# A channel shuffle through PSUM: tiles of 24 KB in eight buffers instead of tiles of 32 KB in six

## The chip, the cores and the metric

The kernel runs on one core of a Trainium2 chip. The metric is the device time of one execution in microseconds (us). The profiled span of the core is about 1.8 us shorter than the device time; spans are compared with spans, and times with times.

## The reference

```python
batch, h, w, c = 16, 64, 64, 256          # groups = 8
x = x.reshape(batch, h, w, groups, c // groups)
x = x.transpose(0, 1, 2, 4, 3)            # swap group and channel-in-group
x = x.reshape(batch, h, w, c)
```

Each run of 256 floats is permuted in itself. 67.1 MB are read and 67.1 MB are written.

## The kernel before

A tile of q rows per partition is q KB a partition (one row is 256 floats, 1 KB). Each tile is loaded by a DMA that SyncE (SP) issues. It is permuted in pieces of 8 KB: VectorE copies a piece into PSUM with the permuted access pattern, ScalarE (ACT) copies it back into the same place. Then ScalarE issues the store. The store therefore stands in ScalarE's own instruction stream: while it waits to be issued, ScalarE copies nothing.

```python
_SIZES = [8] + [32] * 14 + [24, 8, 8, 8, 8]      # KB a partition
_BUFS = 6
_PIECE = 8
# ...
for q in _SIZES:
    buf = pool.tile([P, biggest * c], F32, name="buf")
    nc.sync.dma_start(out=buf[:, : q * c], in_=rows(x_flat, first, q))
    for k in range(0, q, _PIECE):
        piece = buf[:, k * c : (k + _PIECE) * c]
        bounce = psum.tile([P, _PIECE * c], F32, name="bounce")
        nc.vector.tensor_copy(
            out=bounce.rearrange("p (i j g) -> p i j g", j=CPG, g=G),
            in_=piece.rearrange("p (i g j) -> p i j g", g=G, j=CPG),
        )
        nc.scalar.copy(out=piece, in_=bounce)
    nc.scalar.dma_start(out=rows(out_flat, first, q), in_=buf[:, : q * c])
    first += P * q
# ... (launch)
```

The semaphores are not in the source: the Tile framework inserts them.

## Time and profile before

| | before |
|---|---|
| device time, median of the first 3 runs | 320.13 us (319.8 to 320.82) |
| profiled span | 317.8 us |
| VectorE busy / ScalarE busy | 72% / 38% |
| DMA engines at work (packet durations summed, over 16) | 312.4 us |

From the page of the kernel before: the 40 slices of the span (busy tenths; GB/s moved), the chain that ended last, and the two costly groups (busy us, mean ns of one, then idle us just before them and what ended it).

```profile
...
DVE  3199999893975939679395893939849497980471
...
DMA  8999999999999999999999999999999999999995
GB/s 330 406 434 413 429 429 449 408 458 417 445 429 429 445 412 458 400 462 425 433 434 425 449 408 454 429 437 429 429 446 412 442 443 438 418 417 439 413 403 215
...
DVE 59%; DMA 23%; another core or an unknown queue 15%; issue 1%; ACT 1%; SPq 0%; DVEq 0%
...
L54 DVE COPY bounce<-buf 128x2048 f32<-128x2048 f32 x64 | 228.2, 3633 | 83.0 <-DMA buf<-in_x_dram 83.0
L58 ACT COPY buf<-bounce 128x2048 f32<-128x2048 f32 x64 | 119.4, 1865 | 186.9 <-DVE bounce L54 186.9
...
```

The DMA row stays at 9 until the last slice. VectorE leads the chain, but it waits 83.0 us for loads. So the DMA engines bound the kernel, and with the same bytes to move only the two ends can be shortened.

The end of the kernel before, by stretches of time (columns: stretch in us, its length, busy us and instructions of VectorE, ScalarE and GpSimd, clock, DMA share, GB/s; a packet is counted in the stretch in which it starts, so a share can pass 1):

```profile
...
290.00:306.00 16.00, 6.85 (x2) 1.86 (x1) 0.00 (x0) 1.00 0.97 414
306.00:310.00 4.00, 2.71 (x2) 1.86 (x1) 0.00 (x0) 1.00 0.87 367
310.00:314.00 4.00, 1.26 (x1) 1.86 (x1) 0.00 (x0) 1.00 0.40 164
314.00:318.00 4.00, 0.00 (x0) 0.00 (x0) 0.00 (x0) 1.00 0.63 262
...
```

From 310 to 314 us the DMA engines are busy 40%: they wait for VectorE and ScalarE to finish the last small tile before its store can start. The packet records show no packet at all from 311.8 to 314.0 us.

### The profile page before, as it was taken

To read this page: it belongs to the slowest core of one execution; us is meant where nothing else is said; L and a number is where in the kernel's file an instruction comes from. 1 tells how busy PE (TensorE), PEld (TensorE's weight loads), DVE (VectorE), ACT (ScalarE), POOL (GpSimd) and SP (SyncE) were. 2 spreads that over 40 slices of the span, in tenths; PEclk is the share of its full clock that TensorE was granted. 3 is DMA by queue.
4 is the path that set the end of the run, shared out by engine and by line. 5 is a ranking of instruction groups with operands and counts; after the bars stand their busy time and mean duration, and the time that the engine had idled before them with its cause. 6 is when DMAs were issued, how large, how long until landed. Compare 5 with 4: busy or idle time off the path is not lost.

```text
span 317.8 us, 277 instructions
## 1 busy us (share of the span) xinstructions
DVE 228.2 (72%) x64; ACT 120.7 (38%) x65; POOL 0.2 (0%) x4
## 2 busy tenths in 40 slices
DVE  3199999893975939679395893939849497980471
ACT  1225545453351524424244252542505345242222
POOL 0000000000000000000000000000000000000000
DMA  8999999999999999999999999999999999999995
GB/s 330 406 434 413 429 429 449 408 458 417 445 429 429 445 412 458 400 462 425 433 434 425 449 408 454 429 437 429 429 446 412 442 443 438 418 417 439 413 403 215
DMA packets 5762, 134.24 MB, mean 422 GB/s; under 512 B 640, under 2 KB 640, under 8 KB 640
## 3 DMA queue, kind: packets, MB, share of 16 engines
q1 hardware_dynamic: 2880, 67.11, 49.4%
q10 hardware_dynamic: 2880, 67.11, 49.0%
q14 instruction: 2, 0.02, 0.0%
HBM read 67.11 MB, written 67.11 MB: 422 GB/s over the span
## 4 chain that ended last, share of the span: by engine, by line
DVE 59%; DMA 23%; another core or an unknown queue 15%; issue 1%; ACT 1%; SPq 0%; DVEq 0%
DVE bounce L54 59%; DMA buf<-in_x_dram 13%; DMA out_dram<-buf 9%; ACT buf L58 1%; SPq L50 0%; DVEq L54 0%
## 5 line engine op out<-in xcount | busy, mean ns | idle before, releaser
L54 DVE COPY bounce<-buf 128x2048 f32<-128x2048 f32 x64 | 228.2, 3633 | 83.0 <-DMA buf<-in_x_dram 83.0
L58 ACT COPY buf<-bounce 128x2048 f32<-128x2048 f32 x64 | 119.4, 1865 | 186.9 <-DVE bounce L54 186.9
L58 ACT ACT_TABLE_LOAD x1 | 1.3, 1283 | 5.6 <-DMA buf<-in_x_dram 5.6
L77 POOL MEMSET const-bfloat16-1.0<- 128x1 bf16 x1 | 0.1, 102 | 0.0
L77 POOL MEMSET const-uint8-127<- 128x1 uint8 x1 | 0.1, 101 | 0.0
L77 POOL MEMSET const-float32-0.0<- 128x1 f32 x1 | 0.1, 99 | 0.2 <-issue 0.2
L77 POOL MEMSET const-float32-1.0<- 128x1 f32 x1 | 0.1, 98 | 0.0
## 6 DMA issues: line engine op xcount, KB each, us to landing
buf<-in_x_dram SPq DMA_DIRECT2D x14, 4096.0 KB, 61.9
out_dram<-buf ACTq DMA_DIRECT2D x14, 4096.0 KB, 35.7
buf<-in_x_dram SPq DMA_DIRECT2D x5, 1024.0 KB, 35.2
out_dram<-buf ACTq DMA_DIRECT2D x5, 1024.0 KB, 9.9
buf<-in_x_dram SPq DMA_DIRECT2D x1, 3072.0 KB, 59.2
out_dram<-buf ACTq DMA_DIRECT2D x1, 3072.0 KB, 18.8
```

Of the source, the lines that this page charges most:

```text
L54: nc.vector.tensor_copy(out=bounce.rearrange("p (i j g) -> p i j g", j=CPG, g=G), in_=piece.rearrange("p (i g j) -> p i j g", g=G, j=CPG),)
L58: nc.scalar.copy(out=piece, in_=bounce)
L77: nc = _bacc.Bacc("TRN2", target_bir_lowering=False, num_devices=1)
```

## The change

The intent: the same 192 KB a partition, cut into more and finer buffers, and nearly all tiles of one size.

```diff
-_SIZES = [8] + [32] * 14 + [24, 8, 8, 8, 8]
-_BUFS = 6
+_SIZES = [24] * 20 + [8, 24]
+_BUFS = 8
```

## The prediction

> **What bounds the kernel now.** The DMA engines. The page shows their busy share at 9 tenths in every slice but the first and last; they move 433 to 436 GB/s from 100 to 260 us. The Trainium skill ("DMA: Bandwidth & Descriptors", "Where 436 GB/s comes from") puts the ceiling at 435 GB/s: this trace agrees. VectorE is busy 72%, ScalarE 38%. VectorE heads the chain of waits with 59%, but waits 83.0 us for loads: a 32 KB tile costs it 14.26 us, the DMA engines about 19.4 us (load and store). VectorE matters only where the DMA engines run dry.
>
> Summed over the trace's packet records and divided by 16, the DMA engines work 312.4 of the 317.8 us. They start at 1.74 us, lose some 0.5 us on slow first packets, and run dry only after the last load lands (307.6 us): 308 to 311 us partly, 312 to 314 us entirely, some 3 us together.
>
> **What the change does.** Bytes, VectorE and ScalarE work stay the same (64 pieces of 3.63 and 1.87 us). One packet is one partition row of a tile. A 32 KB packet takes 1213 ns, a 24 KB one 912, an 8 KB one 309. Per engine: before 3584x1213 + 256x912 + 1280x309 ns over 16 = 311.0 us; after 5376x912 + 256x309 over 16 = 311.4 us. So +0.4 us, all critical.
>
> Capacity in flight is the same (192 KB a partition), and each 24 KB tile costs VectorE 10.7 us against 14.6 us of DMA. So no starving in the middle. Start: the first load is 3 MB instead of 1 MB, so the first VectorE copy starts near 10 us instead of 5.5, but seven more loads keep the DMA engines busy: no effect.
>
> **The end decides.** Before, the last tile is 8 KB: from landing to store issue 5.6 us, then 1 MB of store. After, the last tile is 24 KB: three copies 10.75 us, ScalarE 1.9, issue and first packet about 1.6, together 14.3 us, then 3 MB of store alone, 7.3 us, and about 1 us to finish. The stores still queued when the last load lands cover it. The Trainium skill (same page, "Queues, rings and completion order") says that an engine round-robins between queue rows packet by packet; the trace agrees: with equal packets both queues get 216 GB/s, and from 270 to 300 us loads of 8 KB packets get about 90 against 340 for the stores of larger packets. Following packets that way with the trace's durations (estimate), one 24 KB and one 8 KB store are left when the last load lands (near 297.5 us): 9.8 us of work. So the DMA engines stand idle about 4.5 us, against 3 before: +1.6 us.
>
> **Sum.** 0.4 + 1.6 = +2.0 us: 322.1 us, range 320.6 to 323.5. Chances: faster by over 2% 0.02, within 2% 0.95, slower 0.03.
>
> **What would show it.** Load and store each near 216 GB/s from 60 to 270 us; packets of 912 ns; VectorE waiting for a load before each tile, some 4 us; the last load landing at 296 to 299 us; one DMA gap of 4 to 5 us just before the last 3 MB store; then 7.3 us of store alone.
>
> **What would make it wrong.** If the store queue held more when the last load lands, the gap closes and the time falls to 318 or less. If 24 KB rows ran at a different speed in bulk than the 256 packets of this trace, every per cent is 3 us. If the load queue empties before stores return buffers, a gap appears near 25 to 60 us.

## The result, and the profile after

| | before | after |
|---|---|---|
| device time, median of 6 runs each | 320.10 us (319.67 to 320.82) | 317.61 us (317.54 to 317.81) |
| ratio | | 0.992 (0.9907 to 0.9934) |
| profiled span | 317.8 us | 315.9 us |
| DMA engines at work | 312.4 us | 313.1 us |
| idle time of the DMA engines after 290 us | 4.0 us | 1.8 us |
| end of the last packet of the last load | 306.9 us | 285.7 us |

A ratio is the mean time of one kernel's fast runs over that of the other's of the same rounds, so it is not quite the ratio of the medians. The last three rows are summed from the trace's packet records.

The change is faster by 0.8%: inside the 2% band, as predicted, but with the opposite sign, and outside the stated range. The same parts of the page after:

```profile
...
DVE  0699999959587685957008986999970299999900
...
DMA  8999999999999999999999999999999999999997
GB/s 296 439 442 380 436 429 433 433 439 433 423 442 433 426 442 426 426 442 426 433 436 427 433 436 436 433 426 437 433 423 448 423 429 444 429 423 433 439 432 302
...
DVE 54%; another core or an unknown queue 23%; issue 8%; ACT 5%; DMA 3%; DVEq 1%; ACTq 0%
...
L54 DVE COPY bounce<-buf 128x2048 f32<-128x2048 f32 x64 | 227.9, 3636 | 72.6 <-ACT buf L58 38.8
L58 ACT COPY buf<-bounce 128x2048 f32<-128x2048 f32 x64 | 119.0, 1866 | 171.1 <-DVE bounce L54 115.3
...
```

and the same stretches at the end:

```profile
...
290.00:306.00 16.00, 10.53 (x3) 7.36 (x4) 0.00 (x0) 1.00 0.98 420
306.00:310.00 4.00, 0.00 (x0) 0.00 (x0) 0.00 (x0) 1.00 1.05 451
310.00:314.00 4.00, 0.00 (x0) 0.00 (x0) 0.00 (x0) 1.00 0.93 399
...
```

The gap before the last store is gone: after 302.5 us no engine computes, and the DMA engines only empty a queue of stores. The DVE row holds something new: two holes of "00" and "02" in mid-kernel, where VectorE stands still although the kernel is faster. The table of waits of the kernel after (engine, line, waited for: us in total, times, longest) says for what:

```profile
...
ACT buf L58 <- DVE bounce L54: 115.3, 56, 5.6
ACT buf L58 <- DMA buf<-in_x_dram: 55.7, 4, 26.0
DVE bounce L54 <- ACT buf L58: 38.8, 4, 18.8
DVE bounce L54 <- DMA buf<-in_x_dram: 33.9, 7, 11.1
...
```

Before, the second and third of these lines do not exist:

```profile
...
ACT buf L58 <- DVE bounce L54: 186.9, 64, 9.7
DVE bounce L54 <- DMA buf<-in_x_dram: 83.0, 18, 7.9
ACT L58 <- DMA buf<-in_x_dram: 5.6, 1, 5.6
...
```

ScalarE's copies read PSUM and need nothing from a later load. Yet ScalarE waits 55.7 us for loads, and VectorE, whose two PSUM buffers are then full, 38.8 us for ScalarE. The longest of these waits in the timeline of the kernel after (start, us, what; in brackets the idle time before it):

```profile
...
136.89 1.86 ACT L58 COPY buf<-bounce 128x2048 f32<-128x2048 f32 x1 [1.68 <-DVE bounce L54]
140.71 7.10 DVE L54 COPY bounce<-buf 128x2048 f32<-128x2048 f32 x2 [3.86 <-DMA buf<-in_x_dram]
164.29 0.34 ACTq L59 DMA_DIRECT2D out_dram<-buf  x1
164.72 3.63 ACT L58 COPY buf<-bounce 128x2048 f32<-128x2048 f32 x2 [25.97 <-DMA buf<-in_x_dram]
...
```

The copies of tile 9 (counted from 0) end at 138.75 us, but its store is issued only at 164.29 us. What it waits for is named in the built program, not in the source. These are lines of its instruction listing, shortened, with the semaphores that each instruction waits for (buf_171 is tile 9, buf_207 is tile 12; the wait for DMAHW2_49 stands in a small instruction just before, and both wait for its value 48, the third landing on it, after the loads of tiles 2 and 7 that of tile 12):

```
DVE  L54 TensorCopy bounce_209<-buf_207 128x2048 [waits DMAHW2_49,Activation_49]
ACT  L59 DMACopy out_0_dram<-buf_171 128x6144 [waits DMAHW2_49,Activation_49]
```

The framework deals eight completion semaphores to the program's 44 DMAs, and a DMA waits until the DMA before it on the same semaphore has landed. The Trainium skill ("DMA: Bandwidth & Descriptors", "Why a DMA increments its semaphore by 16 and not by 1") says why two DMAs in flight must not share one: the count cannot tell whose parts have arrived; "One semaphore per in-flight slot, not one per stream." No run here shows a wrong count, but the trace shows the price of the wait. The store of tile 9 shares its semaphore with the load of tile 12, whose last packet ends at 163.89 us; 0.40 us later the store is issued. The stores of tiles 10, 11 and 15 are held in the same way (by the loads of tiles 13, 14 and 18). In the kernel before, three stores (tiles 8, 9 and 15) share a semaphore with the load of the next tile, but those loads have landed in time: ScalarE waits for no load there except the first.

The theory follows, still to be tested. While stores are held, the loads have the DMA engines to themselves. Summed from packet records, from 150 to 200 us the loads move 253 GB/s and the stores 180. The engines lose nothing meanwhile: their share is 1.01 from 138 to 164 us, during the longest hold. The stores that are kept back are done at the end, where otherwise the engines would stand idle until the last tile is copied. So, by this theory, an accidental wait moved work from where it was plentiful to where it was missing.

Rivals: the queues themselves favour loads with these tile sizes; the 24 KB packets or the eight buffers bring the gain; or long stretches of loads alone, or stores alone, run faster in themselves.

### The profile page after: what moved, and what is told of

Same layout as the page of the kernel before. It is cut to its first block, busy times and chain, and to the rows that moved or that the text cites. A ratio compares the mean times of both kernels' runs of the same rounds, so it can differ in the third digit from the quotient of the medians.

```text
span 315.9 us, 289 instructions
## 1 busy us (share of the span) xinstructions
DVE 227.9 (72%) x64; ACT 120.3 (38%) x65; POOL 0.2 (0%) x4
## 4 chain that ended last, share of the span: by engine, by line
DVE 54%; another core or an unknown queue 23%; issue 8%; ACT 5%; DMA 3%; DVEq 1%; ACTq 0%
DVE bounce L54 54%; ACT buf L58 5%; DMA buf<-in_x_dram 3%; DVEq L91 1%; ACTq L59 0%; DVEq L54 0%; ACTq L58 0%
## 5 line engine op out<-in xcount | busy, mean ns | idle before, releaser
L54 DVE COPY bounce<-buf 128x2048 f32<-128x2048 f32 x64 | 227.9, 3636 | 72.6 <-ACT buf L58 38.8
```

Source lines behind the costliest of these rows:

```text
L54: nc.vector.tensor_copy(out=bounce.rearrange("p (i j g) -> p i j g", j=CPG, g=G), in_=piece.rearrange("p (i g j) -> p i j g", g=G, j=CPG),)
```

## The experiments

All twelve runs gave correct results. They ran in three batches; each batch has its own runs of the kernel before.

| run | what it is | time, us | ratio to before | end of last load, us | DMA idle after 290 us |
|---|---|---|---|---|---|
| e1 | the change, no store shares a semaphore with the load of a later tile | 320.19 | 0.9999 | 294.9 | 4.4 |
| e2 | e1 + store 9 waits for tile 12 by data | 317.78 | 0.9925 | 290.3 | 1.8 |
| e3 | e1 + store 9 waits for tile 11 by data | 320.11 | 0.9996 | 294.7 | 4.4 |
| e4 / e10 | before + store 8 waits for tile 11 by data | 317.72 / 317.80 | 0.9931 / 0.9914 | 302.8 / 301.0 | 3.2 / 1.7 |
| e11 | control of e10 without the wait | 320.00 | 0.9987 | 307.1 | 4.2 |
| e9 | the change again | 317.60 | 0.9926 | 286.1 | 2.0 |
| e5 | e1 with the 8 KB tile last | 317.61 | 0.9926 | 295.0 | 2.1 |
| e6 | the change with six buffers | 320.37 | 1.0007 | 295.0 | 4.7 |
| e8 | sixteen tiles of 32 KB | 318.19 to 320.33 (fast) | 0.9967 | 284.0 | 2.9 |
| e7 | tiles of 16 KB, twelve buffers | 321.52 | 1.0038 | 272.1 | 4.2 |
| e12 | tiles of 16 KB, eight buffers, as e1 dealt | 318.76 | 0.9948 | 296.7 | 1.6 |

About 1.1 to 1.4 us of the last column is the time from the last packet to the end of the span, which every kernel has.

### e1: the same instructions, other semaphores

```diff
-    with _tile.TileContext(nc) as tc:
+    with _tile.TileContext(nc, schedule_with_timeline_sim=True) as tc:
```

The option makes the framework order its bookkeeping by another estimate. The instructions of every engine are the same and in the same order (the two built programs were compared); only the semaphores are dealt differently, so that the store of tile 9 waits for nothing but its own copies. The expectation below says that a store never shares a semaphore with a load. The built program is not quite so: most stores share one with a load, but with that of their own or an earlier tile, which has landed, so no store waits for a load. The waits of the loads change too (in the kernel after, the loads of tiles 6 and 7 wait for those of tiles 1 and 2, 21.5 us in all; in e1 no load waits for a load), so e1 alone does not single out the held stores; e2 and e10 put a single hold back.

> The changed kernel with every instruction in the same order on every engine; only the completion semaphores are dealt out differently, so that a store never shares one with a load. Theory (some stores of the changed kernel are held back until a later load on the same semaphore has landed; that keeps stores for the end): without the holds ScalarE never waits for a load before a store, the last load's last packet ends near 297 us instead of 285.7, the DMA engines stand idle 4 to 5 us before the last 3 MB store, span 319.5 to 320.7 us, time 321.3 to 322.4 us, ratio to before about 1.005. Rival (the DMA queues themselves favour loads, or the tile size alone shifts work to the end; the semaphores do not matter): time stays 317.6 us, ratio 0.992, last load near 286 us.

Measured: 320.19 us. The gain is gone, and the rival that knows no semaphores, with its 317.6 us, falls. In the table of waits of e1, ScalarE waits for no load except the first (11.3 us); VectorE waits 78.9 us for loads again; the gap is back:

```profile
...
DVE bounce L54 <- DMA buf<-in_x_dram: 78.9, 17, 11.3
ACT buf L58 <- DMA out_dram<-buf: 13.8, 2, 6.9
ACT L58 <- DMA buf<-in_x_dram: 11.3, 1, 11.3
...
```

```profile
...
290.00:306.00 16.00, 9.68 (x3) 3.73 (x2) 0.00 (x0) 1.00 0.98 421
306.00:310.00 4.00, 1.03 (x1) 1.86 (x1) 0.00 (x0) 1.00 0.40 168
310.00:314.00 4.00, 0.00 (x0) 0.00 (x0) 0.00 (x0) 1.00 0.92 393
314.00:318.00 4.00, 0.00 (x0) 0.00 (x0) 0.00 (x0) 1.00 0.69 295
...
```

The time fell short of the 321.3 us expected: the gap before the last store, from packet to packet, is 2.4 us (307.4 to 309.8), not 4 to 5. A likely cause lies at the start. The first store is issued at 23.93 us, but its first packet starts at 27.84 us, 3.9 us later; until then the engines move packets of loads alone. The only figure on record for issue and first packet is the prediction's 1.6 us, given for the last store. If it stood for the first store too, loads ran alone for 2.3 us more than allowed; that would bring the last load 2.3 us forward (measured: 294.9 us, not 297) and leave 2.3 us more of stores for the end: a gap of 4.5 - 2.3 = 2.2 us, an estimate from these figures. The packet records of e1 agree: when the last load ends, 12.0 us of issued stores are left, where the prediction had 9.8. No run moves the first store alone, so this is argued, not shown. Two stores of e1 do wait for an earlier store (13.8 us of ScalarE in total), while other stores stand in the queue.

### e2 and e3: one hold put back by data

On top of e1 the loads are written a few tiles ahead in the source, and one line is added before the store (e3 has 11 in place of 12):

```diff
+_HOLDS = {9: 12}
 ...
+        if n in _HOLDS:
+            touch = spare.tile([P, 1], F32, name=f"touch{n}")
+            nc.scalar.copy(out=touch, in_=bufs[_HOLDS[n]][:, :1])
         nc.scalar.dma_start(out=rows(out_flat, firsts[n], q), in_=buf[:, : q * c])
```

> The semaphores of e1, and one hold put back by data: ScalarE copies one column of tile 12 before it issues the store of tile 9 (tiles counted from 0). Theory: this one hold is enough; the last load ends near 288 us, no idle gap before the last store, span 315.3 to 316.3 us, time 317.0 to 318.0 us, about 4 us less than e1. Rival (something else in how e1 was built, not the missing hold, costs time): no better than e1, near 321.5 us.

> As e2, but the store of tile 9 waits for tile 11 instead of tile 12, so the hold is shorter. Theory: about 2 us of stores are kept back instead of 8 to 9; the last load ends near 295 us, a gap of 2 to 3.5 us remains, span 317.5 to 318.8 us, time 319.3 to 320.6 us: between e1 and e2. Rival (the gain does not depend on how many stores are kept back): equal to e1 or to e2.

Measured: e2 317.78 us, as the change; one hold is enough. Two sizes missed: the last load ended at 290.3 us, not 288, and e2 is 2.4 us below e1, not 4, since e1 came out lower. The first has a cause in the built program: the dealing of e2 differs from that of e1 and lets the load of tile 16 wait for that of tile 15, so it is issued at 204.4 us instead of 159.6, and from 204 to 208 us almost only stores move (429 GB/s, loads 3). That gives back about 4 of the 8.9 us by which the hold delays store 9, and it works against the gain, not for it. The table of waits of e2, and its end:

```profile
...
ACT touch L75 <- DMA buf<-in_x_dram: 25.5, 1, 25.5
...
```

```profile
...
306.00:310.00 4.00, 0.00 (x0) 0.00 (x0) 0.00 (x0) 1.00 1.06 457
310.00:314.00 4.00, 0.00 (x0) 0.00 (x0) 0.00 (x0) 1.00 0.91 393
...
```

e3, 320.11 us, lies in its expected range, but no longer between e1 and e2, because e1 came out lower than expected: it is equal to e1. By the words of the expectation that is what the rival said; but e3 turned out to be no test of a shorter hold, for it kept no store back. ScalarE waited 16.4 us for tile 11 there, and it bought nothing. The packet records say why: store 8 was still moving until 157.9 us, and store 9 started at 158.7 us, as in e1 (159.0 us). In e2 it started at 167.8 us. So a hold keeps stores back only as far as it outlasts the stores already queued. ScalarE's waiting time is not the measure of it.

### e4, e10 and e11: the hold alone, in the kernel before

The tiles and buffers of the kernel before, with the loop and the option of e2 and `_HOLDS = {8: 11}`; in e11 `_HOLDS = {}`.

> The kernel before (its tiles, its six buffers), with one hold: ScalarE copies one column of tile 11 before it issues the store of tile 8. Theory: the gap of the kernel before at 308 to 314 us closes, the last load ends near 302 us instead of 307, span 314.6 to 315.8 us, time 316.4 to 317.8 us, ratio to before 0.988 to 0.993: the whole gain of the change without its tile sizes. Rival (the gain comes from tiles of 24 KB or from eight buffers): 320 us, ratio 1.0.

> The kernel of e4 again (the profiled run of e4 was its slowest, 319.15 us against 317.5 to 317.8 in the others), beside its own control. Theory: 317.3 to 318.0 us, ratio to before 0.990 to 0.994, no gap before the last store. Rival (e4's gain is chance or comes from the rewritten loop): as its control.

> The control of the run before: the same rewritten loop and dealing of semaphores, the tiles and buffers of the kernel before, and no hold. Theory: as the kernel before, 319.6 to 320.6 us, ratio 0.998 to 1.002, last load near 307 us, idle 312 to 314 us. Rival (the rewriting itself saves time): as the kernel with the hold, near 317.7 us.

Measured: e4 317.72 us. Its profiled run was its slowest (319.15 us; the other three 317.49 to 317.83), so its packets are not typical; e4's ratio, 0.9931, missed its expected upper end by 0.0001 with that run in it. e10 repeats it: 317.80 us, ratio 0.9914 (0.9893 to 0.9935), against 320.00 us for its control e11, in which the gap is there as before (no packet from 312.1 to 314.4 us). No store waits for a load through a shared semaphore in either of these programs; the waits of their loads are not quite alike (SyncE waits 75.0 us for loads in e10, 103.8 in e11), and no run tests that alone. The end of e10:

```profile
...
306.00:310.00 4.00, 0.00 (x0) 1.86 (x1) 0.00 (x0) 1.00 1.01 426
310.00:314.00 4.00, 0.00 (x0) 0.00 (x0) 0.00 (x0) 1.00 0.92 389
...
```

So the whole gain of the change is to be had in the kernel before, with its tiles and its six buffers, by one wait. The rival that credits 24 KB tiles or eight buffers falls.

### e9, e5, e6 and e8: last tile, buffers, tile size

e9 is the change once more, as the yardstick. e5 is e1 with `_SIZES = [24] * 21 + [8]`. e6 is the change with `_BUFS = 6`. e8 has `_SIZES = [32] * 16` and `_BUFS = 6`.

> The changed kernel once more, on the chip of this batch, as the yardstick for the others: 317.4 to 317.9 us, ratio to before 0.991 to 0.994.

> The tiles of the change with the 8 KB tile last instead of last but one, and the semaphores of e1, so no store is held for a load. Theory (only the idle gap before the last store counts, however it is closed): the last load lands near 295 us, the stores that wait then cover the 5.6 us until the small tile's store is issued, no gap, span 315.3 to 316.3 us, time 317.0 to 318.0 us, ratio about 0.992, as the change. Rival (the held stores save time in themselves, for example because long stretches of pure loads or stores run faster): about 320 us, as e1.

> The tiles of the change, six buffers instead of eight, the default dealing of semaphores. With six buffers the loads that share a semaphore with a later store have landed long before that store is ready, so no hold binds. Theory: as e1, ScalarE waits for no load before a store, the last load near 295 us, a gap of about 2 us before the last store, 319.6 to 320.6 us. Rival (the gain comes from the bytes in flight): clearly slower than e1, since only 144 KB a partition are in flight, 322 us or more.

> A version that may beat both: sixteen tiles of 32 KB, six buffers, no small tiles at all. No hold binds; the first store starts later than in the kernel before (its first tile is four times as large), so the loads get ahead at the start and stores are left over for the end. Estimate from packet times of 1213 ns: 310.5 us of DMA work against 311.4, last load near 283 to 287 us, no gap, span 314.3 to 315.4 us, time 316.0 to 317.2 us, ratio 0.987 to 0.991. If the larger last tile leaves a gap before its 4 MB store, the time is 318 us or more instead.

e5, 317.61 us, equals e9, 317.60 us, with no store held. Its waits of ScalarE and its end:

```profile
...
ACT buf L58 <- DVE bounce L54: 171.2, 64, 6.1
ACT L58 <- DMA buf<-in_x_dram: 10.9, 1, 10.9
...
```

```profile
...
290.00:306.00 16.00, 10.97 (x4) 7.46 (x4) 0.00 (x0) 1.00 1.02 438
306.00:310.00 4.00, 0.00 (x0) 0.00 (x0) 0.00 (x0) 1.00 1.00 430
310.00:314.00 4.00, 0.00 (x0) 0.00 (x0) 0.00 (x0) 1.00 0.85 363
...
```

ScalarE waits for no load except the first. Its last load ends at 295.0 us, as in e1, but its last tile needs one copy instead of three, so the queued stores suffice. Holding stores has therefore no merit of its own; only the gap counts, and there are two ways to close it. The rival of faster one-way stretches falls.

e6, 320.37 us, equals e1 in time, last load and gap. With six buffers no hold binds, and 48 KB a partition less in flight (144 KB against 192) does no further harm. What the eight buffers of the change did shows in the built programs: with six, four stores (tiles 6, 7, 8 and 17) share a semaphore with the load of the next tile, which has landed in time; with eight, the load is up to three tiles ahead, and the store has to wait.

e8 missed. No hold bound and its profile shows no gap before the last store, but its fast runs took 318.19 to 320.33 us, and three of six runs are slow (323.41 to 329.60 us, over 1.5% above its fastest), which no other kernel of the batch has. In its profiled run the last store took 12.1 us (303.4 to 315.5) where the one before took 10.9, and the DMA share falls to 0.53 from 312 to 314 us. Why is left open; it does not beat the change.

### e7 and e12: too many holds

e7 has `_SIZES = [16] * 32` and `_BUFS = 12`; e12 the same tiles, `_BUFS = 8` and the option of e1.

> Tiles of 16 KB, twelve buffers (192 KB a partition as before), the default dealing of semaphores: many stores share a semaphore with a load three to seven tiles ahead and are held until it lands. Theory (a hold is only worth as much as the gap it fills; more of it leaves so many stores for the end that they come out one by one, each waiting for its copies): last load already near 275 us, ScalarE waits for loads again and again, several idle gaps of 1 to 3 us after 300 us, span 321 to 324 us, time 323 to 326 us, slower than before. Rival (keeping stores back is good in itself): below 319 us.

> Tiles of 16 KB with eight buffers instead of twelve, and the semaphores dealt so that no store shares one with a load. Theory: no holds, last load near 297 to 300 us, no idle gap, span 316.9 to 318.2 us (16 KB packets cost about 1.4 us more DMA time than 24 KB ones), time 318.6 to 320.0 us: some 4 to 6 us less than with twelve buffers and holds. Rival (the slowness of 16 KB tiles is their packets or their fixed costs, not the holds): as with twelve buffers, or slower for having fewer.

Measured: e7 321.52 us, slower than before, but less so than expected (323 to 326 us). e12 318.76 us with four buffers fewer. In e7's table of waits, and at its end:

```profile
...
ACT buf L58 <- DMA buf<-in_x_dram: 73.4, 5, 24.1
DVE bounce L54 <- ACT buf L58: 55.2, 4, 20.1
...
```

```profile
...
290.00:306.00 16.00, 16.00 (x5) 8.35 (x5) 0.00 (x0) 1.00 0.95 408
306.00:310.00 4.00, 4.00 (x2) 1.86 (x1) 0.00 (x0) 1.00 1.02 430
310.00:314.00 4.00, 0.30 (x1) 1.86 (x1) 0.00 (x0) 1.00 0.46 197
...
```

All loads have ended at 272.1 us. VectorE, which lost 55.2 us waiting for ScalarE, is still copying without a pause from 290 to 310 us, and the store queue runs dry behind it. The reading is that here the holds have moved too much: the end depends on VectorE again. e7 and e12 differ in buffers as well as in holds, so they do not separate the two; that fewer buffers alone made e12 faster is unlikely, for e6 saw no gain from fewer.

## Why the prediction was right or wrong

- **The DMA engines bound the kernel: right.** They worked 313.1 of 315.9 us. The 435 GB/s that the prediction cites is the section's figure for the SBUF ports; for transfers between HBM and SBUF, as here, the section names a lower limit, that of HBM, and the measured 433 to 436 GB/s lie above it.
- **Packets: right.** "+0.4 us" was predicted from 1213, 912 and 309 ns; the packet medians after are 912 and 309 ns. The measured work rose by 0.8 us (312.38 to 313.14). Not foreseen: more slow load packets early in the kernel (up to 2347 ns instead of 912) cost each engine 1.8 us on average, against 1.4 us before.
- **Loads and stores share the engines packet by packet: right.** The Trainium skill ("DMA: Bandwidth & Descriptors", "Queues, rings and completion order") has the engines alternate between queues packet by packet. This agrees: in the kernel before, 8 KB loads against larger stores moved 78 and 355 GB/s from 280 to 290 us; after, with equal packets, both moved 216 to 217 from 60 to 130 us.
- **"No starving in the middle", first tile "no effect": right for the time of the DMA engines, wrong for the order.** They did not idle in the middle. But the first store came later (packets from 27.7 us, against 15.0 us before), so more of the early time went to loads; from issue to first packet it took 3.9 us there, where the prediction has "about 1.6" at the end, and without holds (e1) the gap was 2.4 us in place of "about 4.5". That the first is the cause of the second is argued, not shown.
- **"One 24 KB and one 8 KB store are left when the last load lands (near 297.5 us): 9.8 us of work": this is the step that failed.** The last load ended at 285.7 us, and 28.4 us of store work was then left, 21.1 us without the last tile's store, where the prediction had 9.8; so the engines were busy to the end. The prediction let every store go as soon as its last copy was done. Four stores were held for a later load on the same semaphore, which e1 (holds away: 320.19 us) and e2 (one hold back: 317.78 us) show to be the cause. Without them "+1.6 us" would have been about +0.4 us (idle time after 290 us: 4.4 in e1 against 4.0 before), so even without the holds the predicted 322.1 us was too high: e1, with 320.19 us and a ratio of 0.9999, lies just under the stated range.
- **The sum.** Between the two profiled runs, +0.8 us of DMA work, and 2.7 us less idle time (of that 2.2 us after 290 us), is the -2.0 us of the spans. Predicted was +0.4 and +1.6.
- **The list of what would make it wrong held the right case**, "if the store queue held more when the last load lands, the gap closes and the time falls to 318 or less", but not its cause. The cause could be read before the run: the instruction listing of the built program names the semaphore of each wait. Only the order of the instructions was looked at.

## What to carry to other kernels

In this kernel, bound by DMA with as much to store as to load, the time that was left lay at the end: what counted was whether enough stores were still queued when the last load landed to cover the copying of the last tile. A small last tile after large ones closed that gap (e5); so did holding a store back once in mid-kernel (e2, e10). A small last tile is not enough by itself: the kernel before ends in four tiles of 8 KB and has the gap. With more holds, e7 had a new gap. When tiles, buffers or order change, read the semaphores of the built program as well as its instructions: DMAs of different queues that share one wait for each other, and the waits move with every change of size.

## What the Trainium skill lacked or had wrong

- "DMA: Bandwidth & Descriptors" ("Why a DMA increments its semaphore by 16 and not by 1") asks for one semaphore per slot in flight, but no page says that a program with more DMAs than semaphores ties DMAs of different queues together. Here eight semaphores for 44 DMAs made ScalarE wait 55.7 us for loads that it did not need.
- The same page ("Latency and other measured facts") gives about 600 ns to the first byte. With an empty queue the trace has 0.84 us from issue to first packet (the last store of e1: 308.96 to 309.80). With loads queued on the same DMA engines it was 3.9 us (first store of e1, 23.93 to 27.84; of the kernel before, 11.07 to 14.95). The page has no figure for this case.
- No page mentions slow load packets early in a kernel: up to 2347 ns instead of 912 in the kernel after, 0.95 us per engine in the first 5 us and 0.76 us from 20 to 60 us.
